# Down-projection of a hybrid decoder layer: tokens of each group loaded in the middle of the group before, VectorE's last group in program order, an early square root

## The chip, the cores and the metric

The kernel runs on one core of a Trainium2 chip. The metric is the device time of one execution in microseconds (us); the profiled execution is one more run of the same program, with the hardware profiler on.

## The reference, cut to what matters

One layer for 2048 tokens of width 1024: a mixer (attention beside a state-space scan, with an output projection), then a SwiGLU feed-forward of inner width 2816, each with a gated residual, and a last RMSNorm:

```python
h = modulate(rmsnorm(x, norm2_w[layer]), shift2, scale2)
x = x + gate2[:, None, :] * swiglu(h, w_gate_up[layer], w_down[layer])
return rmsnorm(x, final_norm_w)
```

The change touches the last two of these lines: the product with `w_down` (2816 to 1024), the residual and the last norm. All products are f32, each made of three matmuls on a high and a low part of both operands.

## The kernel before, in words

Tokens stand in four blocks `b` of 512. The feed-forward runs in two halves: the gate and up products of blocks 0 and 1 (`quads(0, ...)`) write their activations to DRAM (`act_d`), then `down(0)` and `down(1)` multiply them with `w_down`; then the same for blocks 2 and 3: `quads(1, ...)`, `down(2)`, `down(3)`. Beside `down(0)` and `down(1)` run side jobs: the output projection of block 3 (`out_proj`, PE rows `at<-mo,w` and `am<-mo,w`, its weights `w<-w_o`), and the operands of `quads(1)` (`operands_first`, `operands_between`, `operands_last`: SP loads of `mid` at L868, VectorE at L869, L875, L896, L905, L907, L909).

`down(b)` takes the 2816 inner features in six groups `g`: five of 4 chunks of 128, the last (group 5) of 2 chunks. Their order is 0, 1, 5, 2, 3, 4, in block 3 it is 0 to 5. A group goes through eight columns `c` (128 output features each): 12 matmuls of 512 tokens per column (6 in group 5), whose sum leaves one of four PSUM banks `d` through VectorE at L1018 (`x2[c] += gate2 * ps`). `acts(b, g, dn)` brings a group's tokens: SP loads each chunk into a buffer `t` (L991), ScalarE makes the high part (L993), VectorE and GpSimd in turn the low part (L844), into one of eight pairs `a`. The buffers `t` are eight in all (`TMP`), and the loads of `mid`, of the residual `x` and the results on their way out use them too. Weights: SP loads `raw` (L855, five buffers), ScalarE splits (L849), VectorE or GpSimd makes the low part (L850) into `w` (six buffers).

```python
act = acts_ahead.pop(b) if b in acts_ahead else acts(b, g, dn)
```

So in the program a group's tokens stand right ahead of its first column; only block 1 (and 3) has its group 0 loaded at column 3 of the last group of the block before, and block 2 ahead of the last quad. The order in which the engines issue is not the program's: outside a `manual_schedule` region a scheduler with a model of its own orders every engine's queue, SP's too, and each queue then runs in that order and waits at its head.

The norm of blocks 0 to 2 (`final`) runs in columns 0 and 2 of group 0 of the next block (`norm_of_block_before`). In block 3, group 5 is done in two halves of 256 tokens; each half ends with its sums of squares (L1025, by matmul), `quick_root` (L305 to L311, ScalarE's square root at L307), `spread` (L317 on VectorE, L319 on PE) and eight scaled columns (L1035) with their stores (L1036).

Of the kernel before, what the change touches and what calls it, by code (L numbers as in the profile page):

```python
# [17 lines left out]
P = 128  # L18
# [24 lines left out]
def hymba_layer(ctx, tc, xT, crow, pos, wada, wadk, vecs, rows, wq, wkv, wz, wx, wo, wgu, wd4, wd2, outT):  # L43
# [24 lines left out]
    def side_bank(i):  # L68
        return bank(("am", "at", "sm", "st")[i], 1)
# [928 lines left out]
    def down(b, dn, x_pool):  # L998
        x2 = []

        def residual():
# [4 lines left out]
        for at_group, g in enumerate(order):  # L1006
            n = G if g < 5 else NF - 5 * G
            act = acts_ahead.pop(b) if b in acts_ahead else acts(b, g, dn)
            acc = sums() if at_group == 5 and b < NB - 1 else None
# [19 lines left out]
            def final(ts, acc, last=False):  # L1029
                y = rstd(acc[:, ts], st=side_bank(2)) if b < NB - 1 else quick_root(acc, ts.stop // P - ts.start // P, x_pool)  # L1030
                yield
                bc = spread(y, bc=side_bank(3))
                for d in range(KT):
                    x, o = x2[d][:, ts], tmp()[:, ts]
                    nc.vector.scalar_tensor_tensor(o, x, fw_[:, d:d + 1], bc, ALU.mult, ALU.mult)  # L1035
                    (nc.scalar if last and d % 2 else nc.sync).dma_start(outT[b, d][:, ts], o)  # L1036
                yield

            whole = slice(0, T)
            if g < 5:  # L1040
                for c in range(KT):
# [3 lines left out]
                    if at_group == 0 and c in (0, 2):  # L1045
                        norm_of_block_before(b)
                    if at_group == 5 and c == 3 and b % 2 == 0:
                        acts_ahead[b + 1] = acts(b + 1, 0, dn)
                    yield
# [3 lines left out]
            ws = [halves(load_w(wd2[c]), nc.gpsimd if c % 2 else nc.vector) for c in range(4)]  # L1053
            parts = (slice(0, T // 2), slice(T // 2, T)) if b == NB - 1 else (whole,)
            for part, ts in enumerate(parts):
                if b == NB - 1:
                    acc = side_bank(part)
                for c in range(KT):
                    columns(c, ts, ws[c // 2], c % 2 * n * P, acc)
                    yield  # L1060
                if b == NB - 1:
                    drain(final(ts, acc, part == 1))

# [307 lines left out]
    with tc.tile_pool(name="b1", bufs=1, reuse_waits="tile") as bp, ExitStack() as late:  # L1371
# [12 lines left out]
        def next_acts():  # L1384
            acts_ahead[2] = acts(2, 0, dn)
        for i, _ in enumerate(quads(1, ops, lambda f: [side_bank(i) if f % 2 else dense() for i in range(4)], 0, next_acts)):
# [70 lines left out]
```

## Time and profile before

| | |
|---|---|
| median of 3 runs | 2386.41 us (2384.29 to 2386.79) |
| profiled execution | 2389.45 us |
| its span | 2387.7 us |
| busy: PE / weight loads / VectorE / ScalarE / GpSimd | 2252.6 / 1864.8 / 1469.9 / 958.4 / 1240.9 us |
| mean granted TensorE clock | 0.975 |
| share of DMA queue 1 (16 engines) | 52.7% |

The span reaches from the first to the last instruction of the profiled execution; its own time is 1.75 us longer. Busy times of PE are modelled, so a busy PE is not one at its peak. A granted clock of 1.00 is 2.4 GHz, 0.50 is 1.2 GHz, and a stretch's value is the mean over it.

### The profile page before, as it was taken

To read this page: it belongs to the slowest core of one execution; us is meant where nothing else is said; L and a number is where in the kernel's file an instruction comes from. 1 tells how busy PE (TensorE), PEld (TensorE's weight loads), DVE (VectorE), ACT (ScalarE), POOL (GpSimd) and SP (SyncE) were. 2 spreads that over 40 slices of the span, in tenths; PEclk is the share of its full clock that TensorE was granted. 3 is DMA by queue.
4 is the path that set the end of the run, shared out by engine and by line. 5 is a ranking of instruction groups with operands and counts; after the bars stand their busy time and mean duration, and the time that the engine had idled before them with its cause. 6 is when DMAs were issued, how large, how long until landed. Compare 5 with 4: busy or idle time off the path is not lost.

```text
span 2387.7 us, 33182 instructions
## 1 busy us (share of the span) xinstructions
PE 2252.6 (94%) x11292; PEld 1864.8 (78%) x11292; DVE 1469.9 (62%) x2549; ACT 958.4 (40%) x1999; POOL 1240.9 (52%) x1227
## 2 busy tenths in 40 slices
PE   6788989999998899999999999987999999999998
PEld 5578788788878688887888777766788888888787
DVE  8887975673575855766665353597655444554544
ACT  4454543654255555333343232334333333333332
POOL 2756434453222755777874332546666666653431
PEclk9899999999999899999999999999999999999999
DMA  8898987678874422333235765574422222263451
GB/s 291 286 326 301 310 250 243 232 253 266 279 257 143 126 84 71 106 97 93 89 104 167 244 208 167 192 245 146 132 92 78 86 84 80 80 224 102 150 160 58
DMA packets 249065, 412.22 MB, mean 173 GB/s; under 512 B 22464, under 2 KB 68544, under 8 KB 248896
## 3 DMA queue, kind: packets, MB, share of 16 engines
q1 hardware_dynamic: 248320, 409.58, 52.7%
q8 instruction: 89, 1.46, 0.2%
q14 instruction: 80, 0.66, 0.1%
q10 hardware_dynamic: 576, 0.52, 0.1%
HBM read 315.58 MB, written 94.44 MB: 172 GB/s over the span
## 4 chain that ended last, share of the span: by engine, by line
PE 43%; DVE 3%; DMA 1%; issue 1%; POOL 1%; ACT 1%; SPq 0%; DVEq 0%; ACTq 0%; POOLq 0%
PE d L275 5%; PE d L277 5%; PE d L276 5%; PE d L918 5%; PE d L920 5%; PE d L919 5%; PE am L918 1%; PE am L920 1%; PE am L919 1%; PE sm L920 1%; PE sm L918 1%; PE sm L919 1%; PE am L275 1%; DVE t L869 1%; PE am L277 1%
## 5 line engine op out<-in xcount | busy, mean ns | idle before, releaser
L849 ACT ACTIVATE w<-raw 128x512 fp32r<-128x512 f32 x308 | 193.2, 630 | 453.8 <-PE d L277 241.7
L919 PE MATMUL d<-b,w 128*128 128x512 f32 x924 | 368.3, 399 | 2.4 <-POOL b L880 2.4
L920 PE MATMUL d<-b,w 128*128 128x512 f32 x924 | 367.2, 400 | 2.8 <-DVE w L850 2.8
L918 PE MATMUL d<-b,w 128*128 128x512 f32 x924 | 367.0, 401 | 2.6 <-ACT t L941 1.2
L275 PE MATMUL d<-a,w 128*128 128x512 f32 (+1 forms) x720 | 280.6, 397 | 25.1 <-ACT a L993 16.7
L277 PE MATMUL d<-a,w 128*128 128x512 f32 (+1 forms) x720 | 283.2, 394 | 0.0
L276 PE MATMUL d<-a,w 128*128 128x512 f32 (+1 forms) x720 | 281.5, 391 | 0.3 <-POOL a L844 0.2
L850 DVE TENSOR_TENSOR w<-raw,w 128x512 fp32r<-128x512 f32 x220 | 217.0, 989 | 76.6 <-ACT w L849 73.1
L850 POOL TENSOR_TENSOR w<-raw,w 128x512 fp32r<-128x512 f32 x88 | 121.7, 1384 | 246.5 <-ACT w L849 235.3
L1018 DVE SCALAR_TENSOR_TENSOR x<-d,mod,x 128x512 f32<-128x512 f32 (+1 forms) x182 | 131.2, 724 | 173.0 <-PE d L277 170.4
L920 PEld LDWEIGHTS d<-b,w 128*128 128x128 f32 x924 | 175.0, 189 | 43.6 <-DVE w L850 3.2
L919 PEld LDWEIGHTS d<-b,w 128*128 128x128 f32 x924 | 175.6, 190 | 42.5 <-POOL b L880 3.5
L918 PEld LDWEIGHTS d<-b,w 128*128 128x128 f32 x924 | 175.2, 190 | 42.4 <-ACT b L879 1.5
L850 POOL TENSOR_TENSOR w<-s,w 128x512 fp32r<-128x512 f32 x132 | 189.9, 1439 | 26.9 <-ACT w L849 25.7
L849 ACT ACTIVATE w<-s 128x512 fp32r<-128x512 f32 x176 | 111.1, 633 | 209.8 <-PE d L920 156.9
L275 PEld LDWEIGHTS d<-a,w 128*128 128x128 f32 x720 | 136.4, 190 | 62.2 <-ACT a L993 20.0
L275 PE MATMUL d<-w,hl 128*128 128x256 f32 (+1 forms) x592 | 174.7, 295 | 4.5 <-ACT hl L326 2.3
L277 PE MATMUL d<-w,hl 128*128 128x256 f32 (+1 forms) x592 | 169.8, 287 | 0.3 <-DVE hl L327 0.3
L276 PE MATMUL d<-w,hl 128*128 128x256 f32 (+1 forms) x592 | 169.9, 287 | 0.0
L276 PEld LDWEIGHTS d<-a,w 128*128 128x128 f32 x720 | 137.1, 190 | 32.2 <-POOL a L844 0.8
L277 PEld LDWEIGHTS d<-a,w 128*128 128x128 f32 x720 | 136.5, 190 | 30.7 <-issue 0.5
L934 POOL TENSOR_TENSOR s<-raw,s 128x512 f32<-128x512 f32 x44 | 58.1, 1321 | 188.0 <-DVE w L850 113.9
(383 smaller groups left out, 5459.8 us busy)
## 6 DMA issues: line engine op xcount, KB each, us to landing
raw<-in_wgu_dram SPq DMA_DIRECT2D x176, 256.0 KB, 2.7
raw<-in_wd_dram SPq DMA_DIRECT2D x176, 256.0 KB, 2.8
w<-w_x SPq DMA_DIRECT2D x48, 512.0 KB, 5.2
w<-w_o SPq DMA_DIRECT2D x48, 512.0 KB, 4.6
act<-t SPq DMA_DIRECT2D x88, 256.0 KB, 2.1
t<-act SPq DMA_DIRECT2D x88, 256.0 KB, 4.3
t<-in_xT_dram SPq DMA_DIRECT2D x80, 256.0 KB, 4.3
aw<-in_wada_dram SPq DMA_DIRECT2D x64, 256.0 KB, 4.2
```

The costliest lines, as they stand in the source:

```text
L275: nc.tensor.matmul(out, ahi, bhi, start=first, stop=False)
L276: nc.tensor.matmul(out, ahi, blo, start=False, stop=False)
L277: mm3.last = nc.tensor.matmul(out, alo, bhi, start=False, stop=last)
L849: nc.scalar.activation(hi, x, AF.Copy)
L850: eng.tensor_tensor(lo, x, hi.bitcast(F32), ALU.subtract)
L869: nc.vector.scalar_tensor_tensor(x, x, scl2[:, d:d + 1], bc[j], ALU.mult, ALU.mult)
L918: nc.tensor.matmul(out, ahi, bhi, start=first and k == 0, stop=False, skip_group_check=True)
L919: nc.tensor.matmul(out, ahi, blo, start=False, stop=False, skip_group_check=True)
L920: mm3.last = nc.tensor.matmul(out, alo, bhi, start=False, stop=k == 3, skip_group_check=True)
L934: nc.gpsimd.tensor_tensor(s4, a12, s2, ALU.subtract)
L1018: nc.vector.scalar_tensor_tensor(x, ps, gate2[:, c:c + 1], x, ALU.mult, ALU.add)
```

## The change

Three edits. In every group, after column 3, the tokens of the next group are asked for (`next_tokens`, up to group 0 of the next block in blocks 0 and 2). The last group of block 3 stands in a region in which VectorE keeps the program's order, and that order is written out: the root of the first half after column 2 of the second half, four scaled columns of the first half after column 7 of the second, the other four behind the second half's `spread`, which gets another bank (`sm`). And `down(3)` begins with a square root of one column of the identity matrix.

```diff
@@ -997,6 +997,8 @@
 
     def down(b, dn, x_pool):
         x2 = []
+        if b == NB - 1:
+            nc.scalar.activation(small([P, 1], "first_root", 1, pool=x_pool), ident[:, 0:1], AF.Sqrt)
 
         def residual():
             c = len(x2)
@@ -1005,7 +1007,16 @@
         order = (0, 1, 2, 3, 4, 5) if b == NB - 1 else (0, 1, 5, 2, 3, 4)
         for at_group, g in enumerate(order):
             n = G if g < 5 else NF - 5 * G
-            act = acts_ahead.pop(b) if b in acts_ahead else acts(b, g, dn)
+            act = acts_ahead.pop((b, g)) if (b, g) in acts_ahead else acts(b, g, dn)
+
+            def next_tokens():
+                if at_group < 5:
+                    to = b, order[at_group + 1]
+                elif b % 2 == 0:
+                    to = b + 1, 0
+                else:
+                    return
+                acts_ahead[to] = acts(*to, dn)
             acc = sums() if at_group == 5 and b < NB - 1 else None
 
             def columns(c, ts, w, at, sq=None):
@@ -1028,12 +1039,17 @@
 
             def final(ts, acc, last=False):
                 y = rstd(acc[:, ts], st=side_bank(2)) if b < NB - 1 else quick_root(acc, ts.stop // P - ts.start // P, x_pool)
-                yield
-                bc = spread(y, bc=side_bank(3))
+                if b < NB - 1:
+                    yield
+                bc = spread(y, bc=side_bank(2 if last else 3))
+                if b == NB - 1:
+                    yield
                 for d in range(KT):
                     x, o = x2[d][:, ts], tmp()[:, ts]
                     nc.vector.scalar_tensor_tensor(o, x, fw_[:, d:d + 1], bc, ALU.mult, ALU.mult)
                     (nc.scalar if last and d % 2 else nc.sync).dma_start(outT[b, d][:, ts], o)
+                    if b == NB - 1:
+                        yield
                 yield
 
             whole = slice(0, T)
@@ -1044,22 +1060,35 @@
                     columns(c, whole, halves(load_w(wd4[g, c]), nc.gpsimd if c % 2 else nc.vector), 0, acc)
                     if at_group == 0 and c in (0, 2):
                         norm_of_block_before(b)
-                    if at_group == 5 and c == 3 and b % 2 == 0:
-                        acts_ahead[b + 1] = acts(b + 1, 0, dn)
+                    if c == 3:
+                        next_tokens()
                     yield
                 if acc is not None:
                     finish_of[b] = final(whole, acc)
                 continue
             ws = [halves(load_w(wd2[c]), nc.gpsimd if c % 2 else nc.vector) for c in range(4)]
-            parts = (slice(0, T // 2), slice(T // 2, T)) if b == NB - 1 else (whole,)
-            for part, ts in enumerate(parts):
-                if b == NB - 1:
+            if b < NB - 1:
+                for c in range(KT):
+                    columns(c, whole, ws[c // 2], c % 2 * n * P)
+                    if c == 3:
+                        next_tokens()
+                    yield
+                continue
+            with tc.manual_schedule(engines={mybir.EngineType.DVE}):
+                ends = []
+                for part, ts in enumerate((slice(0, T // 2), slice(T // 2, T))):
                     acc = side_bank(part)
-                for c in range(KT):
-                    columns(c, ts, ws[c // 2], c % 2 * n * P, acc)
-                    yield
-                if b == NB - 1:
-                    drain(final(ts, acc, part == 1))
+                    ends.append(final(ts, acc, part == 1))
+                    for c in range(KT):
+                        columns(c, ts, ws[c // 2], c % 2 * n * P, acc)
+                        if part and c == 2:
+                            next(ends[0])
+                        yield
+                for i in range(KT // 2):
+                    next(ends[0])
+                next(ends[1])
+                drain(ends[0])
+                drain(ends[1])
 
     def norm_of_block_before(b):
         if b - 1 in finish_of:
@@ -1382,7 +1411,7 @@
                     sides.append(last)
         finish(last)
         def next_acts():
-            acts_ahead[2] = acts(2, 0, dn)
+            acts_ahead[2, 0] = acts(2, 0, dn)
         for i, _ in enumerate(quads(1, ops, lambda f: [side_bank(i) if f % 2 else dense() for i in range(4)], 0, next_acts)):
             if i in (0, 2):
                 norm_of_block_before(2)
```

Line numbers move: L1018 becomes L1029, L1035 L1049, L1036 L1050, L1025 L1036, L1004 L1006. The scheduler's order of the queues moves at these places; of blocks 2 and 3, SP's queue (the loads of tokens among them) keeps the order it had, row for row.

**Block 1, start of group 3.** SP before, with the loads of tokens (L991) of groups 3 and 4, of `mid` (L868) and of weights (L855):

```order
L868 DMA t<-mid_211 128x512
L868 DMA t<-mid_210 128x512 x2
L855 DMA raw<-in_wd_dram 128x512 x2
L991 DMA t<-act_216 128x512 x8
L855 DMA raw<-in_wd_dram 128x512 x5
L855 DMA raw<-in_wgu_dram 128x512 x12
```

and with the change, the same place, where the first L991 rows are those of group 3:

```order
L868 DMA t<-mid_211 128x512
L855 DMA raw<-in_wd_dram 128x512 x2
L868 DMA t<-mid_211 128x512 x2
L868 DMA t<-mid_210 128x512 x2
L855 DMA raw<-in_wd_dram 128x512 x2
L991 DMA t<-act_216 128x512 x3
L855 DMA raw<-in_wd_dram 128x512 x2
L991 DMA t<-act_216 128x512
L868 DMA t<-mid_211 128x512 x2
```

The tokens of group 3 now stand ahead of eight more weight loads and of the last twelve loads of `mid`; before, all loads of `mid` were ahead of them. VectorE before, from the last column of group 2 (`x_15529`) to the first of group 3 (`x_15295`):

```order
L1018 SCALAR_TENSOR_TENSOR x_15529<-d,mod,x_15529 128x512
L907 SCALAR_TENSOR_TENSOR t<-t,mod 128x512
L869 SCALAR_TENSOR_TENSOR t<-t,scl_148,at 128x512
L869 SCALAR_TENSOR_TENSOR t<-t,scl_148,am 128x512 x2
L909 SCALAR_TENSOR_TENSOR t<-t,mod 128x512
L905 SCALAR_TENSOR_TENSOR t<-t,dsh 128x512
L844 TENSOR_TENSOR a<-t,a 128x512
L907 SCALAR_TENSOR_TENSOR t<-t,mod 128x512
L875 SCALAR_TENSOR_TENSOR b<-t,mod,b 128x512
L909 SCALAR_TENSOR_TENSOR t<-t,mod 128x512
L844 TENSOR_TENSOR a<-t,a 128x512 x3
L1018 SCALAR_TENSOR_TENSOR x_15295<-d,mod,x_15295 128x512
```

and with the change, from the same column (`x_15549`) to one behind the first of group 3 (`x_15295`, `x_15351`):

```order
L1029 SCALAR_TENSOR_TENSOR x_15549<-d,mod,x_15549 128x512
L869 SCALAR_TENSOR_TENSOR t<-t,scl_148,am 128x512
L905 SCALAR_TENSOR_TENSOR t<-t,dsh 128x512
L1029 SCALAR_TENSOR_TENSOR x_15295<-d,mod,x_15295 128x512
L869 SCALAR_TENSOR_TENSOR t<-t,scl_148,at 128x512
L850 TENSOR_TENSOR w<-raw,w 128x512
L909 SCALAR_TENSOR_TENSOR t<-t,mod 128x512
L1029 SCALAR_TENSOR_TENSOR x_15351<-d,mod,x_15351 128x512
```

Of 13 instructions ahead of that first column two are left; the others stand between other columns, on both sides. Instructions of 128x512 on VectorE up to each group's last column in block 1, before and now: group 1 41 and 31 (with 18 and 8 of 128x4 or 128x128), group 5 18 and 22, group 2 31 and 32, group 3 25 and 28, group 4 12 and 12.

**Block 0, output projection beside it.** PE before, in the middle of an output column (`at_14822`), which takes two weight tiles of 12 matmuls each:

```order
L276 MATMUL at_14822<-mo_14414,w_14823 128x512
L277 MATMUL at_14822<-mo_14414,w_14823 128x512
L275 MATMUL at_14822<-mo_14435,w_14875 128x512
L276 MATMUL at_14822<-mo_14435,w_14875 128x512
L277 MATMUL at_14822<-mo_14435,w_14875 128x512
```

and now:

```order
L276 MATMUL at_14822<-mo_14414,w_14823 128x512
L277 MATMUL at_14822<-mo_14414,w_14823 128x512
L275 MATMUL d_14842<-a_14633,w_14839 128x512
L276 MATMUL d_14842<-a_14633,w_14839 128x512
L277 MATMUL d_14842<-a_14633,w_14839 128x512
```

Before, the two halves stood back to back; now 24 matmuls of the down-projection stand between them. Two other such pairs were 24 in a row, and are split too.

**The last half group.** VectorE before, at the end of the second half's last column (`x_21069`):

```order
L1035 SCALAR_TENSOR_TENSOR t<-x_21006,vec,st 128x256
L1035 SCALAR_TENSOR_TENSOR t<-x_21027,vec,st 128x256
L1035 SCALAR_TENSOR_TENSOR t<-x_21048,vec,st 128x256
L1035 SCALAR_TENSOR_TENSOR t<-x_21069,vec,st 128x256
L1018 SCALAR_TENSOR_TENSOR x_21069<-d,mod,x_21069 128x256
L305 TENSOR_SCALAR qr<-at 128x2
```

and now (`x_21091` is the same column):

```order
L1029 SCALAR_TENSOR_TENSOR x_21091<-d,mod,x_21091 128x256
L1049 SCALAR_TENSOR_TENSOR t<-x_20873,vec,st 128x256
L1049 SCALAR_TENSOR_TENSOR t<-x_20914,vec,st 128x256
L1049 SCALAR_TENSOR_TENSOR t<-x_20935,vec,st 128x256
L1049 SCALAR_TENSOR_TENSOR t<-x_20987,vec,st 128x256
L305 TENSOR_SCALAR qr<-at 128x2
```

The last column now stands ahead of all scaled columns of the first half instead of behind them. ScalarE's new square root and its table stand in the last quad, where a tanh (L972) follows:

```order
L849 ACTIVATE w<-raw 128x512
L1001 ACT_TABLE_LOAD
L1001 ACTIVATE first_root<-ident 128x1
L849 ACTIVATE w<-raw 128x512 x3
L972 ACT_TABLE_LOAD
L972 ACTIVATE t<-t 128x512
```

and in the last half group, where `x_20933` is column 2 of the second half:

```order
L1034 ACTIVATE s<-x_20935 128x256
L307 ACT_TABLE_LOAD
L307 ACTIVATE qr<-qr 128x2
L1034 ACTIVATE s<-x_20987 128x256
L1034 ACTIVATE s<-x_21028 128x256
```

ScalarE thus loads three tables from here on, where the kernel before loads one, at L307: the load at the end stays where it was, behind column 2.

## Rows read from the trace of the kernel before

**Rows 1.** PE's waits, whole span: waiting line, released by: us, times, longest.

```profile
PE d L275 <- ACT a L993: 16.7, 5, 12.0
...
PE at L1025 <- ACT s L1023: 2.7, 1, 2.7
PE at L275 <- DMA w<-w_o: 2.7, 1, 2.7
```

**Rows 2.** Busy time by stretch: block 0, block 1 (two), blocks 2 and 3.

```profile
core 0: us, PE busy (x) PEld busy (x) DVE busy (x) ACT busy (x) POOL busy (x), PEclk, DMA share, GB/s
...
1420.00:1460.00 40.00, 37.33 (x155) 29.87 (x154) 10.85 (x15) 8.22 (x13) 8.42 (x7) 0.96 0.59 181
...
1572.00:1625.00 53.00, 47.58 (x194) 35.67 (x194) 53.00 (x75) 22.36 (x38) 27.93 (x18) 1.00 0.62 194
1625.00:1638.00 13.00, 0.97 (x5) 0.50 (x4) 13.00 (x18) 3.81 (x7) 10.18 (x7) 0.72 0.72 222
...
2110.00:2240.00 130.00, 130.00 (x564) 105.58 (x563) 65.08 (x88) 47.31 (x79) 58.80 (x43) 1.00 0.51 155
2240.00:2280.00 40.00, 36.67 (x147) 28.49 (x146) 24.57 (x43) 12.23 (x20) 13.43 (x11) 0.91 0.68 216
```

**Rows 3.** Timeline of PE at the start of group 3, block 1.

```profile
1625.32 0.39 PE L277 MATMUL d<-a,w 128*128 128x512 f32 x1
1637.74 1.65 PE L275 MATMUL d<-a,w 128*128 128x512 f32 x3 [12.03 <-ACT a L993]
```

**Rows 4.** Timeline of SP's queue there.

```profile
1631.14 1.45 SPq L855 DMA_DIRECT2D raw<-in_wd_dram  x2
1632.81 11.41 SPq L991 DMA_DIRECT2D t<-act  x8
```

**Rows 5.** Timeline of VectorE: last columns of groups 0, 1 and 4, block 1.

```profile
1558.75 0.74 DVE L1018 SCALAR_TENSOR_TENSOR x<-d,mod,x 128x512 f32<-128x512 f32 x1
...
1593.76 0.74 DVE L1018 SCALAR_TENSOR_TENSOR x<-d,mod,x 128x512 f32<-128x512 f32 x1
...
1684.53 0.75 DVE L1018 SCALAR_TENSOR_TENSOR x<-d,mod,x 128x512 f32<-128x512 f32 x1 [2.02 <-PE d L277]
```

**Rows 6.** VectorE by line, 1572 to 1641 us: count, busy us, mean ns.

```profile
L850 DVE TENSOR_TENSOR w<-raw,w 128x512 fp32r<-128x512 f32 x10 | 9.8, 982 | 0.0
...
L909 DVE SCALAR_TENSOR_TENSOR t<-t,mod 128x512 f32<-128x512 f32 x4 | 4.4, 1095 | 0.0
```

**Rows 7.** Timeline of VectorE, the last 15 us.

```profile
2373.71 3.22 DVE L1035 SCALAR_TENSOR_TENSOR t<-x,vec,st 128x256 f32<-128x256 f32 x8 [0.64 <-PE st L319]
2376.85 0.48 DVE L1018 SCALAR_TENSOR_TENSOR x<-d,mod,x 128x256 f32<-128x256 f32 x1
2378.66 0.16 DVE L305 TENSOR_SCALAR qr<-at 128x2 f32<-128x2 f32 x1 [1.33 <-PE at L1025]
...
2379.49 0.16 DVE L310 SCALAR_TENSOR_TENSOR qr<-qr 128x2 f32<-128x2 f32 x1
2379.68 0.16 DVE L311 SCALAR_TENSOR_TENSOR qr<-qr 128x2 f32<-128x2 f32 x1
...
2381.67 3.22 DVE L1035 SCALAR_TENSOR_TENSOR t<-x,vec,st 128x256 f32<-128x256 f32 x8 [1.31 <-PE st L319]
```

**Rows 8.** Timeline of PE, last matmul of the last column.

```profile
2373.68 0.28 PE L277 MATMUL d<-a,w 128*128 128x256 f32 x1
```

**Rows 9.** Timeline of ScalarE: last quad, and the last half group.

```profile
2109.43 0.63 ACT L849 ACTIVATE w<-raw 128x512 fp32r<-128x512 f32 x1 [0.73 <-PE st L920]
...
2116.20 0.63 ACT L972 ACTIVATE t<-t 128x512 f32<-128x512 f32 x1
2118.21 0.63 ACT L849 ACTIVATE w<-raw 128x512 fp32r<-128x512 f32 x1 [1.38 <-PE am L920]
...
2368.83 1.28 ACT L307 ACT_TABLE_LOAD   x1
```

**Rows 10.** VectorE by line, 2140 to 2240 us.

```profile
L850 DVE TENSOR_TENSOR w<-raw,w 128x512 fp32r<-128x512 f32 x18 | 14.1, 786 | 0.0
```

## The prediction

> **What bounds the kernel now.** I read PE's waits first, then busy time by stretch, then the timelines of the places found. PE's waits [rows 1] show few holes behind this change's code: 16.7 us in five waits for the high part of a group's tokens (L993), one of them 12.0 us; 2.7 us for a weight tile of the output projection; 2.7 us for a square (L1023) in the last half group. The stretches [rows 2] give PE's pace where nothing waits: 564 matmuls in 130 us, 0.2305 us each, so a column of 12 takes 2.77 us, one of group 5 1.38 us. Against that pace three stretches fall short. In block 0 (1420 to 1460) 155 matmuls stand where 173.5 fit: 18.5 x 0.2305 = 4.3 us lost. In blocks 2 and 3 (2240 to 2280) 147 stand: 6.1 us lost. The large loss is in block 1: from the last column of group 0 at 1558.75 to that of group 4 at 1684.53 [rows 5] pass 125.8 us, and the 432 matmuls between (36 columns' worth) need 99.6. 26.2 us are lost there, in two forms. From 1572 to 1625 VectorE is busy 53.00 of 53.00 us and sets the pace [rows 2]; from 1625.32 to 1637.74 PE stands still for group 3's tokens [rows 3], which SP issues at 1632.81 [rows 4], behind weight loads that wait for free weight buffers and behind all loads of `mid` for the next half. The granted clock in that stretch is 0.72 [rows 2], between its levels of 1.2 and 2.4 GHz; it fell after PE had stood still.
>
> **Block 1, the main term.** The same VectorE instructions run before and after; what moves is where they stand. Price of one, from group 1, which VectorE paced: 1593.76 - 1558.75 = 35.0 us [rows 5] for 41 instructions of 128x512 and 18 small ones; small ones start 0.2 us apart (L310 and L311) [rows 7], so (35.0 - 3.6)/41 = 0.766 us. With the change a group takes the longer of PE's time and VectorE's count. Group 1: 31 x 0.766 + 8 x 0.2 = 25.3. Group 5: 22 x 0.766 = 16.9 (PE: 11.1). Group 2: 32 x 0.766 = 24.5. Group 3: 28 x 0.766 = 21.4, so PE's 22.2. Group 4: 22.2. Sum 111.1; against 125.8 the gain is **14.7 us**. The hole of 12.4 us goes because the loads of group 3 leave SP eight weights and twelve `mid` loads earlier, about a group ahead of need, and because VectorE has two instructions ahead of group 3's first column where it had 13. Late next is VectorE itself, in groups 1, 5 and 2, by 3.1 + 5.8 + 2.3 us over PE. Bounds: PE's pace alone gives 26.2 less some 0.5 us for two spreads (L319), a gain of 25.7. Above, at 0.85 us each: 27.9 + 18.7 + 27.2 + 23.8 + 22.2 = 119.8, a gain of 6.0. The trace shows L850 at 982 ns and L909 at 1095 ns in this stretch [rows 6], so contention with GpSimd is in my price, but only as much as it was.
>
> **Block 0.** Its 4.3 us go with one wait, on the second weight tile of an output column whose halves stood back to back [rows 1]. Now 24 matmuls, 5.5 us, stand between, and two weight tiles are no longer asked for at once. I take 4 us; bounds 0, if the load is late elsewhere, and 4.3. Group 1's tokens are loaded earlier too, where PE waited under 1 us.
>
> **Blocks 2 and 3.** Nothing: SP's queue there is what it was, so the loads of group 1 of block 3 still stand behind the stores of block 2's result, and the 6.1 us stay. This is where the change does not do what it says.
>
> **The last half group.** The last column's matmul starts at 2373.68 and lasts 0.28 [rows 8], so VectorE could take it at 2373.96; it takes it at 2376.85, behind eight scaled columns in 3.22 us [rows 7]. With the change it goes first: 2.9 us. Four matmul instructions of the square sums move behind it on PE, some 0.4 us more. Against it: four scaled columns (1.6 us at 0.40 each) now stand between the last column and L305, where VectorE idled 1.33 us, 0.3 us over; the other four stand where it idled 1.31 us waiting for the spread, 0.3 us over. ScalarE's table at L307 (1.28 us [rows 9]) stays, so the early root buys nothing. Sum 2.7, I take **2.5 us**; bounds 1.5 (VectorE's columns 3 to 6 now wait behind the whole first root) and 3.3.
>
> **The early root.** It adds two table loads to ScalarE in the last quad, 1.28 us each [rows 9] and 0.2 for the root. The first stands ahead of a weight split that waited 0.73 us anyway, the second ahead of the tanh at 2116.20, after which ScalarE idled 1.38 us. Weights are split several columns ahead and PE is busy 130 of 130 us [rows 2]; I cost it nothing. If the cover is gone it is 2 x 1.28 + 0.2 = 2.8 us.
> The Trainium skill, "ScalarE: Activation LUTs", What ACT_TABLE_LOAD costs, adds a drain to each switch of set, 2.66 us in all. By it the uncovered cost would be 5.5 us; the root here starts 1.30 us after its load.
>
> **Sum.** 14.7 + 4 + 2.5 = 21.2 us. The profiled execution took 2389.45 us, so 2368.3 for one like it; that execution is 3.04 us above the median of the runs, 2386.41, so the runs should give **2365.2 us**.
>
> **Rivals.**
> VectorE becomes the bound (slower). Tokens' low parts, weights' low parts and the operands of the next half now run in the same columns on VectorE and GpSimd. If that makes each of the 113 instructions of groups 1, 5, 2 and 3 cost what L909 costs in the crowded stretch, 1.095 us [rows 6], the groups take 113 x 1.095 + 1.6 + 22.2 = 147.5 us, 21.7 more than before; with 6.5 us won elsewhere that is 15.2 us slower, 2401.6. It decides from a mean of 0.96 us on. For it: L850's 982 ns. Against it: the whole of group 1 came to 0.766 with the same mix, and GpSimd was busy 27.93 of 53 us there [rows 2].
> The Trainium skill, "SBUF — State Buffer", Who interferes with whom, says that a VectorE instruction with two SBUF inputs and a GpSimd one that reads SBUF exclude each other, whichever starts first. By that rule more overlap means more such waits; the trace agrees that the same instruction costs more in the crowded stretch: L850 takes 982 ns there [rows 6] and 786 in block 2 [rows 10].
>
> The wait moves (smaller gain). Tokens loaded early hold four of the eight buffers `t`, and loads of `mid` and of output weights queue behind them on SP. If new holes take back block 1's gain whole, 6.5 us are left: 2379.9. For it: the buffers are few. Against it: a group's buffers are freed as soon as its split is done, and in the new order a group's pairs `a` are free by then.
>
> The change does what it says in block 3 too (larger gain): the 6.1 us go as well, 2359.1. Against it: the queue's rows.
>
> Nothing measurable: time won in block 1 is waited for at the start of the second quads, whose operands are VectorE's. 2386. Against it: the last of them (L909) stands nine columns, 25 us, ahead of the end of group 4.
>
> **How the numbers follow.** What a measurement can tell from no change is about 0.2%, 4.8 us. Forecast, with its bounds: 0.80. The wait moves: 0.08. VectorE as bound: 0.05. Block 3 too: 0.04. Nothing: 0.03. Faster by over 0.2%: 0.80 + 0.08 + 0.04 = 0.92; within it 0.03; slower 0.05. Range: the low end takes the best bounds, 25.7 + 4.3 + 3.3 = 33.3, so 2353; the high end the worst, 6.0 + 0 + 1.5 = 7.5, so 2379, and one more for the case in which the wait moves: 2380.
>
> **What would show it.** Right: no wait of PE over 4 us on L993 in block 1; from the last column of group 0 to that of group 4 some 111 us, with VectorE full in groups 1 to 2; no wait on `w_o`; the hole of block 3 still there; three table loads at the end; the last column's VectorE step directly behind its matmul. Wrong: if block 1 is over 120 us, my price or the queues are; if the end gains less than 1.5 us, the root's place is; if PE waits in the last quads, the table loads are not covered.

## The result, and the profile after

The changed kernel took 2370.93 us (median of 4 runs, 2369.56 to 2373.64) beside 2386.60 for the kernel before: a ratio of 0.9937, 95% interval 0.992 to 0.9955, so 15.7 us faster. A second set of runs of both gave 2373.99 against 2386.25, a ratio of 0.995 (0.9936 to 0.9963), 12.3 us. The prediction was 2365.2, range 2353 to 2380: the direction and the range held, the gain of 21.2 us was 5.5 to 9 us too large.

The profiled execution of the change took 2371.23 us (span 2369.5, mean granted clock 0.980). PE's waits behind the changed code, whole span (columns as in [rows 1]):

```profile
PE d L275 <- DVE x L1029: 13.3, 9, 3.9
...
PE d L275 <- ACT a L993: 3.9, 3, 2.9
```

and the first of these lines in the kernel before:

```profile
PE d L275 <- DVE x L1018: 8.2, 8, 2.9
```

The waits for tokens fell from 16.7 us to 3.9, and their longest from 12.0 to 2.9; in block 0 PE no longer waits for `w_o`. The wait on VectorE's emptying of the PSUM banks (L1018 before, L1029 now) grew from 8.2 us to 13.3. The stretches that answer to [rows 2]:

```profile
core 0: us, PE busy (x) PEld busy (x) DVE busy (x) ACT busy (x) POOL busy (x), PEclk, DMA share, GB/s
1420.00:1460.00 40.00, 40.00 (x175) 32.47 (x174) 12.42 (x18) 9.19 (x16) 11.53 (x9) 1.00 0.57 186
1551.00:1650.00 99.00, 86.36 (x352) 65.92 (x351) 98.73 (x131) 42.81 (x73) 55.69 (x38) 0.98 0.64 205
2110.00:2240.00 130.00, 130.00 (x563) 105.01 (x562) 66.86 (x102) 44.32 (x72) 54.20 (x40) 1.00 0.44 130
2245.00:2255.00 10.00, 7.07 (x25) 5.22 (x25) 6.61 (x10) 2.52 (x4) 2.54 (x2) 0.83 0.99 328
```

Block 0 has no hole left between 1420 and 1460. In block 1 VectorE is busy 98.73 of 99 us, and PE does 352 matmuls where 429 fit. The hole at the start of group 1 of block 3 is still there (7.07 of 10 us busy).

To compare stretches I use VectorE's steps on columns as marks. First column of block 1, last of its group 0, last of its group 4, after:

```profile
1518.30 0.75 DVE L1029 SCALAR_TENSOR_TENSOR x<-d,mod,x 128x512 f32<-128x512 f32 x1 [2.04 <-PE d L277]
...
1555.62 0.74 DVE L1029 SCALAR_TENSOR_TENSOR x<-d,mod,x 128x512 f32<-128x512 f32 x1
...
1669.84 0.75 DVE L1029 SCALAR_TENSOR_TENSOR x<-d,mod,x 128x512 f32<-128x512 f32 x1 [2.03 <-PE d L277]
```

The first of these marks in the kernel before, whose other two are in [rows 5]:

```profile
1525.33 0.75 DVE L1018 SCALAR_TENSOR_TENSOR x<-d,mod,x 128x512 f32<-128x512 f32 x1 [0.85 <-PE d L277]
```

The table has such stretches for all profiled executions, in us. "Block 0" runs from the last column of its group 0 to the first of block 1, "block 1" from there to the last of group 4, "block 2" from its first column to the first of block 3, "block 3" from there to the last column of group 4, "end" from there to the end of the span.

| kernel | block 0 | block 1 | block 2 | block 3 | end |
|---|---|---|---|---|---|
| before | 154.33 | 159.20 | 127.72 | 117.00 | 30.81 |
| the change | 148.08 | 151.55 | 128.75 | 114.47 | 28.45 |
| the change, second set of runs | 148.08 | 152.61 | 128.75 | 114.30 | 28.44 |
| tokens alone | 148.08 | 151.23 | 128.75 | 114.33 | 31.17 |
| end alone | 153.80 | 161.40 | 127.72 | 114.17 | 28.39 |
| no early root | 148.08 | 154.76 | 128.75 | 114.68 | 28.45 |
| block 0 alone | 148.14 | 159.69 | 128.75 | 115.84 | 28.44 |
| fewer operands | 148.08 | 144.61 | 128.75 | 115.18 | 28.56 |
| weights on GpSimd | 148.08 | 152.13 | 128.75 | 114.47 | 29.19 |
| weights on VectorE | 148.08 | 154.37 | 128.75 | 114.94 | 28.45 |
| low parts on ScalarE | 148.08 | 142.78 | 128.75 | 116.43 | 28.45 |
| operands first | 141.70 | 154.27 | 128.74 | 114.97 | 28.41 |
| ratio 0.65 | 154.10 | 166.02 | 127.74 | 115.91 | 28.41 |
| operands first, tokens at column 1 | 137.80 | 154.75 | 127.75 | 110.16 | 28.43 |

Up to the last column of group 0 of block 0, ahead of nearly all that these kernels change, the executions already differ by 7 us (1367.15 to 1374.23); the stretches leave that out.

The change's gain in the two profiles is therefore 6.25 us in block 0, 7.65 in block 1 and 2.36 at the end, less 1.03 in block 2: 15.2 us. Single executions differ in these stretches: the kernel with the new end alone, whose tokens are loaded as before, takes 161.40 us in block 1 for 159.20, so block 1's gain is known to some 2 us. Block 3's 2.5 us are not the change's. The kernel with the end alone has them too. The stretches (columns as above) behind a hole of 3 us, in the kernel before:

```profile
2255.00:2265.00 10.00, 7.32 (x29) 4.96 (x27) 8.65 (x13) 2.28 (x4) 2.53 (x2) 1.00 0.74 230
2265.00:2275.00 10.00, 9.36 (x27) 7.16 (x28) 2.13 (x3) 4.04 (x7) 3.42 (x3) 0.66 1.04 361
```

and in the kernel with the end alone:

```profile
2255.00:2265.00 10.00, 7.50 (x31) 5.46 (x30) 8.01 (x12) 2.52 (x4) 2.53 (x2) 1.00 0.65 214
2265.00:2275.00 10.00, 9.40 (x39) 6.91 (x38) 4.00 (x5) 4.42 (x7) 4.52 (x4) 1.00 1.01 374
```

In the profiled execution of before the granted clock fell to 0.66 behind the hole (27 matmuls in 10 us), with the end alone it stayed at 1.00 (39 matmuls). Block 3 takes 2.8 us more by it. The execution that I worked from stood 3.04 us above the median; that this dip is why is likely, but not shown, since the others of that kernel left no trace.

The end after the change, VectorE (answers to [rows 7]):

```profile
2355.70 1.65 DVE L1029 SCALAR_TENSOR_TENSOR x<-d,mod,x 128x256 f32<-128x256 f32 x4
2357.74 0.48 DVE L1029 SCALAR_TENSOR_TENSOR x<-d,mod,x 128x256 f32<-128x256 f32 x1 [0.40 <-PE d L277]
2358.14 1.65 DVE L1049 SCALAR_TENSOR_TENSOR t<-x,vec,st 128x256 f32<-128x256 f32 x4
2359.87 0.16 DVE L305 TENSOR_SCALAR qr<-at 128x2 f32<-128x2 f32 x1
...
2361.16 0.48 DVE L317 TENSOR_SCALAR t<-ident,qr 128x128 f32<-128x128 f32 x2
2361.55 1.65 DVE L1049 SCALAR_TENSOR_TENSOR t<-x,vec,st 128x256 f32<-128x256 f32 x4
2363.12 3.22 DVE L1049 SCALAR_TENSOR_TENSOR t<-x,vec,sm 128x256 f32<-128x256 f32 x8
```

The last column (2357.74) waits for its own matmul alone, and the eight scaled columns of the first half now lie in two fours where VectorE idled before. From the end of the span: the last column stands 11.77 us ahead of it, before it was 10.88; and it comes 9.25 us behind the first half's last column, before 12.49. The square root's table is still loaded at L307, as foreseen (timeline of ScalarE, the change):

```profile
2352.98 1.28 ACT L307 ACT_TABLE_LOAD   x1
2354.28 0.20 ACT L307 ACTIVATE qr<-qr 128x2 f32<-128x2 f32 x1
```

### The profile page after: what moved, and what is told of

Same layout as the page of the kernel before. It is cut to its first block, busy times and chain, and to the rows that moved or that the text cites. A ratio compares the mean times of both kernels' runs of the same rounds, so it can differ in the third digit from the quotient of the medians.

```text
span 2369.5 us, 33207 instructions
## 1 busy us (share of the span) xinstructions
PE 2245.6 (95%) x11292; PEld 1861.3 (79%) x11292; DVE 1463.7 (62%) x2549; ACT 962.0 (41%) x2002; POOL 1240.4 (52%) x1227
## 4 chain that ended last, share of the span: by engine, by line
PE 43%; DVE 4%; DMA 1%; issue 1%; POOL 1%; ACT 0%; SPq 0%; DVEq 0%; POOLq 0%; ACTq 0%
PE d L275 5%; PE d L276 5%; PE d L277 5%; PE d L918 5%; PE d L920 5%; PE d L919 5%; PE am L920 1%; PE am L918 1%; PE am L919 1%; PE sm L920 1%; PE sm L918 1%; PE sm L919 1%; DVE t L869 1%; PE am L275 1%; PE am L277 1%
## 5 line engine op out<-in xcount | busy, mean ns | idle before, releaser
L275 PE MATMUL d<-a,w 128*128 128x512 f32 (+1 forms) x720 | 282.9, 396 | 17.4 <-DVE x L1029 13.3
L850 DVE TENSOR_TENSOR w<-raw,w 128x512 fp32r<-128x512 f32 x220 | 211.2, 962 | 73.1 <-ACT w L849 69.7
L850 POOL TENSOR_TENSOR w<-raw,w 128x512 fp32r<-128x512 f32 x88 | 121.4, 1380 | 221.8 <-ACT w L849 203.1
L1029 DVE SCALAR_TENSOR_TENSOR x<-d,mod,x 128x512 f32<-128x512 f32 (+1 forms) x182 | 131.0, 724 | 170.9 <-PE d L277 168.0
L850 POOL TENSOR_TENSOR w<-s,w 128x512 fp32r<-128x512 f32 x132 | 190.9, 1448 | 23.2 <-ACT w L849 22.3
```

The costliest lines, as they stand in the source:

```text
L275: nc.tensor.matmul(out, ahi, bhi, start=first, stop=False)
L850: eng.tensor_tensor(lo, x, hi.bitcast(F32), ALU.subtract)
L1029: nc.vector.scalar_tensor_tensor(x, ps, gate2[:, c:c + 1], x, ALU.mult, ALU.add)
```

## The experiments

### Taking the change apart: four kernels

**Tokens alone**: the early tokens, with the end of the kernel before and no early root. The edit against the change, cut:

```diff
-        if b == NB - 1:
-            nc.scalar.activation(small([P, 1], "first_root", 1, pool=x_pool), ident[:, 0:1], AF.Sqrt)
...
-            with tc.manual_schedule(engines={mybir.EngineType.DVE}):
...
+            parts = (slice(0, T // 2), slice(T // 2, T)) if b == NB - 1 else (whole,)
...
```

> Only the earlier tokens; end and square root as before. My theory (the gain is block 1 and 0, the end adds 2.4 us): 2373.3 us, 13.3 below before, and VectorE takes the last column behind eight scaled columns again. Rival (the earlier tokens bring less, the new end more than the trace of its last 15 us shows): 2376 or more.

Measured 2373.65 us beside 2387.45 (ratio 0.9952, 0.9935 to 0.997): 13.8 us below, near the 13.3 of my theory. The "end" is back at 31.17 us.

**End alone**: the end in VectorE's program order, tokens loaded as before, no early root. Against the change, cut:

```diff
-        if b == NB - 1:
-            nc.scalar.activation(small([P, 1], "first_root", 1, pool=x_pool), ident[:, 0:1], AF.Sqrt)
...
             def next_tokens():
-                if at_group < 5:
-                    to = b, order[at_group + 1]
-                elif b % 2 == 0:
+                if at_group == 5 and b % 2 == 0:
                     to = b + 1, 0
```

> Only the new order of the end; tokens as before, no early square root. My theory: 2.4 us below before, 2384.2 us. Rival (the end gains nothing by itself, since the last column's step is late for another reason): 2386.6 us, within 0.5 of before.

2384.46 beside 2387.45 (0.9988, 0.9978 to 0.9999): 3.0 us, and 30.81 to 28.39 at the end in the traces. The two halves come to 16.8 us, beside 15.7 and 12.3 for the whole: within the intervals, nothing is left over.

**No early root**: the two lines of `first_root` left out.

```diff
-        if b == NB - 1:
-            nc.scalar.activation(small([P, 1], "first_root", 1, pool=x_pool), ident[:, 0:1], AF.Sqrt)
```

> The change without the early square root. My theory (its two table loads lie beside other work): 2370.9 us, within 0.7 of the change. Rival (the loads slow the last quads and group 0 of block 2, whose matmuls stood 233.4 ns apart in the change and 231.4 before): 1 to 2.5 us below the change, 2368.4 to 2369.9, and matmuls 231.4 ns apart again in block 2.

2374.07 beside 2387.45 (0.9947, 0.9931 to 0.9963); the change had 0.9937 and 0.995 beside its own runs of before. From block 1's last column to block 2's first pass 428.01 us, with the root 428.00; block 2 is at 128.75 in both, the end at 28.45 in both. So the root costs nothing and buys nothing, and it is not what slows block 2. Block 1 takes 3.2 us more in this execution. Of these 2.6 lie in group 0 (39.95 us for 37.33), where the granted clock fell behind a hole of 3.3 us: 22 matmuls in this stretch, where the change does 32 at 1.00 (busy time by stretch, no early root):

```profile
1540.00:1550.00 10.00, 7.10 (x22) 5.40 (x20) 5.38 (x10) 1.50 (x3) 1.78 (x2) 0.66 1.00 344
```

**Block 0 alone**: early tokens in block 0 alone.

```diff
-                if at_group < 5:
+                if at_group < 5 and b == 0:
                     to = b, order[at_group + 1]
-                elif b % 2 == 0:
+                elif at_group == 5 and b % 2 == 0:
                     to = b + 1, 0
```

> The change with tokens loaded early in block 0 alone; in blocks 1 to 3 as before. My theory (block 0 wins 7 us, group 0 of block 1 waits for VectorE and gives 4 to 5 of it back, the end wins 2.4): 5 to 6 us below before, 2381 us. Rival (block 0's 7 us stay won): 9 to 10 below, 2377 us.

2379.55 beside 2387.45 (0.9964, 0.9951 to 0.9978): 7.9 us below, between the two expectations; the traces decide. Block 0 keeps its 6.2 us, and block 1 takes 159.69 us, 0.5 more than before. My theory that group 0 of block 1 hands block 0's gain back falls: it takes 33.2 us here and 33.4 before. It is longer in the change (from 1518.30 to 1555.62, 37.3 us), so by block 1's own early tokens. Between those marks VectorE has 55 instructions for 43 before, and PE does 141 matmuls for 127: VectorE reaches the group's last column later, with PE already further into group 1.

### What paces block 1: VectorE's count, or time that it shares with GpSimd

Theory 1 is that of my prediction: so many instructions of 128x512 at some 0.77 us, whatever GpSimd does. Theory 2: a VectorE instruction with both inputs in SBUF and one of GpSimd don't run side by side. The change's trace speaks for the second. VectorE by line in the change, 1551 to 1650 us (count, busy us, mean ns, idle before):

```profile
L1029 DVE SCALAR_TENSOR_TENSOR x<-d,mod,x 128x512 f32<-128x512 f32 x34 | 24.8, 738 | 0.0
...
L875 DVE SCALAR_TENSOR_TENSOR b<-t,mod,b 128x512 fp32r<-128x512 f32 x12 | 12.2, 1028 | 0.1
...
L869 DVE SCALAR_TENSOR_TENSOR t<-t,scl,at 128x512 f32<-128x512 f32 x12 | 8.7, 732 | 0.0
...
L905 DVE SCALAR_TENSOR_TENSOR t<-t,dsh 128x512 f32<-128x512 f32 x4 | 5.7, 1412 | 0.0
```

and GpSimd by line, the same stretch:

```profile
L880 POOL TENSOR_TENSOR b<-t,b 128x512 fp32r<-128x512 f32 x16 | 23.2, 1458 | 20.3 <-ACT b L879 20.3
L850 POOL TENSOR_TENSOR w<-raw,w 128x512 fp32r<-128x512 f32 x13 | 20.3, 1563 | 12.3 <-ACT w L849 12.3
```

L1029 and L869 read one input from PSUM (`d`, `at`): 738 and 732 ns. L905 and L875 read both from SBUF (tiles `t`, `b`): 1412 and 1028. The change's timeline of VectorE at one place shows how:

```profile
1633.30 1.78 DVE L905 SCALAR_TENSOR_TENSOR t<-t,dsh 128x512 f32<-128x512 f32 x1
1635.00 1.78 DVE L875 SCALAR_TENSOR_TENSOR b<-t,mod,b 128x512 fp32r<-128x512 f32 x1
1636.70 0.74 DVE L909 SCALAR_TENSOR_TENSOR t<-t,mod 128x512 f32<-128x512 f32 x1
```

and that of GpSimd:

```profile
1632.79 1.74 POOL L880 TENSOR_TENSOR b<-t,b 128x512 fp32r<-128x512 f32 x1
1634.49 1.74 POOL L850 TENSOR_TENSOR w<-raw,w 128x512 fp32r<-128x512 f32 x1
1638.19 2.57 POOL L880 TENSOR_TENSOR b<-t,b 128x512 fp32r<-128x512 f32 x2 [1.95 <-ACT b L879]
```

L905 ends 0.55 us after GpSimd's L880, L850 on GpSimd ends 1.15 us after L905, L875 0.55 us after that. While they alternate, each takes over 1.7 us; L909, with GpSimd idle, takes 0.74. The Trainium skill, "SBUF — State Buffer", Who interferes with whom, states this exclusion, and that a VectorE instruction with at most one SBUF input, outside its 2-port modes, is free of it. The trace agrees on both (1412 against 732 ns). Four kernels test what the exclusion is worth here.

**Fewer operands**: 16 VectorE instructions left out.

```diff
-            nc.vector.tensor_tensor(h[0, 1], h[0, 1], h[0, 0], ALU.subtract)
+            if s == 0:
+                nc.vector.tensor_tensor(h[0, 1], h[0, 1], h[0, 0], ALU.subtract)
...
```

(and the same ahead of L905, L907 and L909).

> The change, with 16 VectorE instructions of 128x512 left out that form four sums and differences of operands for the second half's quads in block 1 (L875, L905, L907, L909); loads, buffers and GpSimd's work as in the change. The output is not the reference's. My theory (VectorE's count paces block 1 at some 0.77 us each): 9 to 12 us below the change, 2359 to 2362 us. Rival (buffers t and SP's queue pace it): within 3 us of the change, 2368 to 2371.

The expectation names L875 for L896, the line that was left out. 2365.29 beside 2383.66 (0.9926, 0.9906 to 0.9947); by the ratios alone this can't be told from the change. In the traces block 1 takes 144.61 us, 6.9 less than the change. The instructions were taken out of groups 2 and 3, and from the last column of group 0 to that of group 3 it takes 82.6 us for 94.2: 11.6/16 = 0.73 us for an instruction, near the 0.77 of theory 1. The rest is given back at both ends, 2.5 us in group 0 (39.8 for 37.3, in an execution whose clock was 0.90 around it) and 2.2 in group 4, which then takes PE's 22.2 us for 20.0. So VectorE's work does pace those groups, which both theories allow. The rival, by which buffers `t` and SP's queue set the pace and under 3 us are won, falls short; more buffers were not tried.

**Weights on GpSimd**: the low parts of block 1's weights all there.

```diff
-                    columns(c, whole, halves(load_w(wd4[g, c]), nc.gpsimd if c % 2 else nc.vector), 0, acc)
+                    columns(c, whole, halves(load_w(wd4[g, c]), nc.gpsimd if c % 2 or b == 1 else nc.vector), 0, acc)
...
```

(and the same for the weights `wd2` of group 5).

> The change, with the low parts of all weights of block 1 on GpSimd (22 instructions less on VectorE, 22 more on GpSimd at some 1.27 us). My theory (VectorE's count is the bound): 6 to 10 us below the change, 2361 to 2365 us. Rival (what VectorE loses is time shared with GpSimd, so that moving work between them wins nothing, or GpSimd becomes the bound): 2370 to 2378 us, VectorE's instructions over 0.85 us in the stretch.

2372.25 beside 2383.66 (0.9955, 0.994 to 0.997). Block 1: 152.13 us, 0.6 more than the change, with a clock of 0.90 around group 0 here too. The rival was right.

**Weights on VectorE**: the other way round.

```diff
-                    columns(c, whole, halves(load_w(wd4[g, c]), nc.gpsimd if c % 2 else nc.vector), 0, acc)
+                    columns(c, whole, halves(load_w(wd4[g, c]), nc.gpsimd if c % 2 and b != 1 else nc.vector), 0, acc)
...
```

(and the same for `wd2`).

> The change, with the low parts of all weights of block 1 on VectorE: 18 or more instructions of some 0.70 us more there, as many of 1.27 us or more less on GpSimd. Theory 1 (VectorE's count at 0.77 us each): 10 to 15 us slower than the change. Theory 2 (the two engines share their time on SBUF, and VectorE uses it up in half the time that GpSimd takes): within 4 us of the change.

2375.06 beside 2386.25 (0.9953, 0.9939 to 0.9967); the change beside the same runs 2373.99. Block 1: 154.37 us, 2.8 more, where theory 1 wanted 10 to 15. These 2.8 come from group 4 alone, which takes 28.8 us for 20.0: PE has a new wait for tokens at its start (PE's waits, 1551 to 1660 us):

```profile
PE d L275 <- ACT a L993: 5.5, 1, 5.5
```

From the last column of group 0 to that of group 3, VectorE has seven more instructions of 128x512 than in the change, 120 for 113, and takes 6.1 us less, 88.1 for 94.2.

**Low parts on ScalarE**: L880 off GpSimd, VectorE's work untouched.

```diff
-    def kept(into, x, eng=nc.gpsimd):
+    def kept(into, x, eng=nc.gpsimd, s=1):
         hi, lo = into
         nc.scalar.activation(hi, x, AF.Copy)
-        eng.tensor_tensor(lo, x, hi.bitcast(F32), ALU.subtract)
+        nc.scalar.activation(lo, x, AF.Copy) if s else eng.tensor_tensor(lo, x, hi.bitcast(F32), ALU.subtract)
...
```

(the callers hand `s` on, so that only the operands of block 1 change).

> The change, with the 16 low parts that GpSimd makes of operands in block 1 (L880, 1.46 us each) replaced by copies on ScalarE (0.63 us); VectorE's instructions as in the change. The output is not the reference's. Theory 1 (VectorE's count alone paces block 1): within 2 us of the change. Theory 2 (a VectorE instruction with both inputs in SBUF and one of GpSimd don't run side by side): those of VectorE fall from 1.03 us towards 0.75 in the stretch, and the kernel is 5 to 9 us below the change.

2364.83 beside 2386.25 (0.991, 0.9894 to 0.9926), 9.2 us below the change beside the same runs; block 1 142.78, 8.8 less. No instruction was taken from VectorE. Theory 2 holds, and theory 1, which wanted a change of under 2 us, falls. Busy time from 1551 to 1650 us (columns as above), with the weights on GpSimd:

```profile
1551.00:1650.00 99.00, 88.52 (x357) 66.71 (x356) 93.96 (x111) 44.36 (x76) 77.47 (x53) 0.98 0.62 195
```

with the weights on VectorE:

```profile
1551.00:1650.00 99.00, 85.13 (x345) 64.59 (x345) 98.86 (x147) 43.08 (x73) 35.69 (x23) 0.95 0.66 209
```

with the low parts on ScalarE:

```profile
1551.00:1650.00 99.00, 94.55 (x397) 73.86 (x397) 97.07 (x137) 54.15 (x95) 40.20 (x27) 1.00 0.65 204
```

VectorE by line in that stretch, with the low parts on ScalarE:

```profile
L875 DVE SCALAR_TENSOR_TENSOR b<-t,mod,b 128x512 fp32r<-128x512 f32 x12 | 9.1, 773 | 0.1
...
L905 DVE SCALAR_TENSOR_TENSOR t<-t,dsh 128x512 f32<-128x512 f32 x4 | 4.0, 998 | 0.0
```

L875 fell from 1028 to 773 ns, L905 from 1412 to 998. VectorE's busy time by its number of instructions (small ones included) follows GpSimd's busy time. The last two columns are what the marks give for the stretch from the last column of group 0 to that of group 3, with VectorE's instructions of 128x512 in it, and for group 4:

| kernel | GpSimd busy, us of 99 | VectorE busy / instructions | groups 1, 5, 2, 3: us, instructions | group 4, us |
|---|---|---|---|---|
| weights on VectorE | 35.69 | 98.86 / 147 = 0.67 us | 88.1, 120 | 28.8 |
| low parts on ScalarE | 40.20 | 97.07 / 137 = 0.71 us | 86.2, 113 | 17.8 |
| the change | 55.69 | 98.73 / 131 = 0.75 us | 94.2, 113 | 20.0 |
| weights on GpSimd | 77.47 | 93.96 / 111 = 0.85 us | 91.1, 99 | 22.2 |

"Fewer operands", whose mix of instructions is another, does not fit this row of means: 65.02 us of GpSimd and 90.20 / 122 = 0.74. Moving a low part from one engine to the other wins little, because both draw on the same time; taking one off both wins. That buffers `t` also come free earlier with the low parts on ScalarE is a part of its 8.8 us that the run can't set apart.

### Versions that might beat both

**Operands first**: the first operands of `quads(1)` ahead of the output projection, beside block 0.

```diff
-        sides.extend([second_output(), first_operands()])
+        sides.extend([first_operands(), second_output()])
```

> The change, with the first operands of the second half formed ahead of the output projection beside block 0, where VectorE is a quarter busy, and not behind it in group 0 of block 1. Theory (group 0 of block 1 is longer by VectorE's work): that group 5 to 9 us shorter than the change's 37.3, 2362 to 2366 us. Rival (the root of block 3's tokens then comes right before the operands that need it, and PE waits for it): a new hole of 3 to 5 us, 2367 to 2370 us.

2367.35 beside 2383.66 (0.9938, 0.9914 to 0.9962): by the ratio no better than the change. In the traces blocks 0 and 1 together take 295.97 us for 299.63; they are taken together because 46 matmuls of the output projection move from the one to the other. Group 0 of block 1 is 1.5 us shorter, not 5 to 9, since matmuls of the output projection now lie in it.

**Ratio 0.65**: side work brought forward in block 0.

```diff
-            for _ in beside(down(b, dn, dn), 0.3 if last else 0.55):
+            for _ in beside(down(b, dn, dn), 0.3 if last else 0.65):
```

> The change, with the side work beside block 0 at 0.65 steps a column for 0.55, so that the last operands begin some eight columns earlier, where VectorE is idle more. Theory: block 1 loses 6 to 10 us of VectorE's time, 2361 to 2365 us. Rival (block 0 fills up instead, or the projection's weights come late again): 2369 to 2374 us.

2396.77 beside 2383.66 (1.0053, 1.0038 to 1.0068): a miss, and slower than the kernel before, by a return of the old wait and one of 10.9 us for VectorE in group 0 (PE's waits, 1518 to 1690 us):

```profile
PE d L275 <- ACT a L993: 18.1, 1, 18.1
PE d L275 <- DVE x L1029: 13.7, 4, 10.9
```

SP issued those tokens at 1618.10, behind loads of `mid` up to 1616.75: the place in the program, which is the change's, did not decide where they stand; the scheduler did.

**Operands first, tokens at column 1**: the version before last, with both `if c == 3: next_tokens()` at column 1; the change itself ran beside it.

```diff
-                    if c == 3:
+                    if c == 1:
                         next_tokens()
```

> The version with the first operands ahead of the output projection, and each group's tokens asked for after column 1, not 3. Theory (group 4 of block 1 waits 7.4 us in that version since its tokens come late): 5 to 10 us below the change, the waits at the start of group 4 under 3 us. Rival (buffers t and VectorE's order hold those tokens up wherever they are asked for): the waits stay, 3 to 5 us below the change.

> The change itself, beside the three other runs of this call: 15 to 16 us below before, as at first. Both theories.

2357.23 us (2355.66 to 2358.67) beside 2386.25: a ratio of 0.9878 (0.9862 to 0.9893), 16.8 us below the change's 2373.99 beside the same runs, and beyond the 5 to 10 expected. In the traces, against the change's first, blocks 0 and 1 together take 7.1 us less, block 2 1.0, block 3 4.3; another 3.1 is the spread ahead of them. PE waits 9.5 us in block 1 (from 1500 to 1660 us, this version; in the change 16.1, of which L1029 has 13.3):

```profile
PE d L275 <- ACT b L879: 3.8, 3, 3.0
PE d L275 <- DVE x L1029: 3.3, 2, 3.1
PE d L276 <- DVE a L844: 2.4, 1, 2.4
```

The theory of the expectation does not explain the gain. The waits at the start of group 4 and shortly behind it are still 3.0 and 2.4 us (the first and last of these lines), and block 1 is no shorter than in "operands first" (154.75 for 154.27 us). What is won over that version lies in block 0 (3.9 us; it waited 2.1 us there for L1029, and this one does not wait), in block 2 (1.0) and in block 3 (4.8), where the hole is gone. Timeline of PE in the change, at the start of group 1 of block 3:

```profile
2247.35 0.40 PE L277 MATMUL d<-a,w 128*128 128x512 f32 x1
2250.68 0.79 PE L275 MATMUL d<-a,w 128*128 128x512 f32 x1 [2.93 <-ACT a L993]
```

and, in this version, busy time in the stretch that holds that group (VectorE's last columns of groups 0 and 1 stand at 2239.1 and 2258.9):

```profile
2235.00:2260.00 25.00, 25.00 (x109) 20.27 (x108) 16.23 (x23) 10.50 (x17) 9.46 (x8) 1.00 0.87 301
```

Asked for at column 1, those tokens are issued ahead of the stores of block 2's result (timeline of SP, this version):

```profile
2212.60 1.85 SPq L991 DMA_DIRECT2D t<-act  x4
...
2233.02 1.65 SPq L1050 DMA_DIRECT2D out_dram<-t  x3
```

At column 3 they stand between and behind them (timeline of SP, the change):

```profile
2244.25 1.65 SPq L1050 DMA_DIRECT2D out_dram<-t  x3
2246.87 0.33 SPq L991 DMA_DIRECT2D t<-act  x1
```

This is the version to keep.

## Why the prediction was right or wrong

**Block 1, 14.7 us predicted, 7.7 measured: the step that failed.** The mechanism was right: the hole for group 3's tokens went, and VectorE became what is waited for (98.73 of 99 us). Two things were mis-sized. I counted from the last column of group 0, but the change also moves work ahead of it: 33.4 us from the block's first column to that one became 37.3, and 3.9 us were given back where I had not looked. And in the counted stretch 114.2 us stand where I had 111.1: groups 26.3, 15.1, 26.8, 26.0 and 20.0 for 25.3, 16.9, 24.5, 22.2 and 22.2. The counts of instructions came out as I had them; the price did not. In group 3 I let PE set the pace, since VectorE's 28 instructions at 0.766 us came to 21.4; VectorE stayed full to its end, and the 28 took 26.0 us, 0.93 each. In group 2 they took 0.84. The 0.766 us was the price of group 1 before and is not a constant: from 1551 to 1650 the change's 117 instructions of 128x512 take up to 98.73/117 = 0.84 us each, and those with two SBUF inputs up to 1.4 in the mean of a line where GpSimd works beside them. The result lies within the bounds that I gave (6.0 to 25.7), near the lower one.

**Block 0, 4 us predicted, 6.2 measured.** The wait on `w_o` went as foreseen. The window I took held the longer of two, with the lower clock behind it (0.96 in the mean of the window), 4.3 us together: PE had also stood from 1403.80 to 1405.03 for another tile of `w_o`, 1.0 us more than a matmul takes. The last 1 us was not traced. That block 0 gave more than foreseen is luck, and made up for a part of what block 1 fell short.

**Block 2: nothing predicted, 1.0 us lost.** Matmuls stand 0.8% farther apart in all of block 2 (128.75 against 127.72 us), the same to 0.01 us in ten executions of nine kernels, and not in the two others with early tokens: ratio 0.65, and tokens at column 1. The early root is excluded, since it is there without the root too. The prediction's reason for nothing was SP's unchanged queue, and that does not cover the pace of PE. The cause stays open.

**Block 3: nothing predicted, nothing found** beyond the clock in the execution of before (0.66 behind the hole, and 26.6 us for the group, for 23.8 at 1.00 with the end alone). Its hole stayed, as the queue's rows said.

**The end, 2.5 predicted, 2.4 measured** (3.0 with the end alone, in medians), by the steps listed: the last column behind its own matmul, two fours of scaled columns in idle time, L307's table where it was.

**The early root, 0 predicted, 0 measured.**

**The rivals.** VectorE did become the bound, but at no more than 0.84 us for each of 128x512 over the stretch, under the mean of 0.96 from which that rival decides; its mechanism, the exclusion with GpSimd, is real and took part of the gain. The wait did move, from tokens to VectorE, but not to buffers `t`, and not the whole gain.

**The reference point.** The profiled execution stood 3.04 us above the median. I took that off the sum, which was right. One dip of the clock in block 3, 2.8 us, is its likely cause, not a shown one.

## What to carry to other kernels

When a stretch is bound by an engine, count its instructions from the start of the stretch in which the moved work can land, not from the first place that the change names: what leaves one group may land in the group ahead. Price VectorE and GpSimd together: instructions with two SBUF inputs on both share time, so moving them between the two wins little, and moving them off both wins. Reading one input from PSUM should win too, by the 0.73 us of such instructions; no kernel here tried it. Where a scheduler sets the queues, an early request in the program is only a wish: look where the loads land, and try neighbouring places: column 1 for column 3 was worth 10.1 us here (2367.35 to 2357.23, in two sets of runs; 10.0 between their traces).

## What the runs showed of the hardware that I had not expected

The granted clock after a hole of some 3 us is not the same in every execution. At the start of group 1 of block 3 two matmuls stood 3.00 us apart before, and the clock was 0.66 from 2265 to 2275; they stood 2.90 us apart with the end alone, and it was 1.00. The group took 26.6 and 23.8 us. The change's hole there is longer than both, 3.33 us, with 0.83 from 2245 to 2255 and 24.2 us. Such a hole thus costs up to some 3 us beyond its length. The change has one in block 1 (1541.87 to 1545.02) and one in block 3 (2247.35 to 2250.68). How much of the spread of its runs (2371.64 to 2377.85 in the second set) comes from them was not tried by itself.

VectorE and GpSimd alternate where both have two SBUF inputs: both instructions are stretched to 1.7 to 1.8 us, from 0.74 (L909 above) and some 1.3 (two of L880 in 2.57 us, above), while L1029 and L869, with one input in PSUM, stay at 0.73 to 0.74 in the mean. With 16 low parts moved from GpSimd to ScalarE, and none of VectorE's instructions, block 1 was 8.8 us shorter.
